# Thirteen ways to pass from the output projection of one block to the input projection of the next

## The chip, the cores and the metric

The kernel runs on one core of a Trainium2 chip. The metric is the device time of one execution in microseconds (us); the median of several runs is compared. TensorE appears in the profile as PE (matmuls) and PEld (weight loads), VectorE as DVE, ScalarE as ACT, GpSimd as POOL, and SyncE, which issues the large DMAs, as SP.

## The reference, cut to what matters

Two layers are computed on 256 rows of 1024 channels. Each layer has a feed-forward network (FFN), a token mixer and a second FFN, so there are four FFNs:

```
def swiglu(x, w_in, w_out):
    gate, up = jnp.split(x @ w_in, 2, axis=-1)
    return (jax.nn.silu(gate) * up) @ w_out

for l in range(2):
    x = layer_norm(alpha * x + 0.5 * swiglu(x, w_ff1_in[l], w_ff1_out[l]), ...)
    x = layer_norm(alpha * x + hybrid_mixer(x, ...), ...)
    x = layer_norm(alpha * x + 0.5 * swiglu(x, w_ff2_in[l], w_ff2_out[l]), ...)
```

The inner width of an FFN is 4096. All of it is float32.

## The kernel before, in words

**Precision.** A float32 product is made of three matmuls of a shorter type. Each operand is split into `hi` and `lo` (line 90 on ACT rounds, line 91 on DVE subtracts), and hi times hi, hi times lo and lo times hi are added up in PSUM. Each matmul has a weight load of its own, of 128 by 128.

**Input projection.** An FFN is cut into 32 units of 128 gate and 128 up columns. For one unit `wide` calls `mm3` sixteen times (two column groups, eight slices of the 1024 channels), so that a unit is 48 matmuls of 256 columns, on lines 185, 186 and 187 in turn. Their output tile is called `mm` or `sm`. `gate` then makes silu(gate) times up, and `split` leaves `g[u]` as a `hi` and a `lo`.

**Output projection.** After every second unit a block `j` follows, which adds the product of `g[2j]`, `g[2j+1]` and two weight tiles to the four accumulators `acc` (two row tiles by two halves of 512 columns). `rows` issues it: 2 units by 2 row tiles by 3 products by 2 halves, 24 matmuls of 512 columns, all on line 203. With `NLAST = 6` there are 13 such blocks in an FFN, 52 in the kernel. Block 12 is followed by four units without a block, and the last six `g` are multiplied in `finish`. The first three units of an FFN (two in the very first) are made in another way, by lines 286 to 288 with transposes on line 253.

**Order.** One list of instructions goes to each engine. A planner puts them in order from the program's order and from when it thinks that an operand is there. In the steady part of an FFN the trace shows the program's own order: 96 matmuls of two units, then 24 of the block, and so on. At the start of an FFN it shows pieces of the first block among the units.

**Data.** `Ring.chunk` fetches 1 MB of weights by a DMA on SP's queue into a tile `raw` and splits it into two pairs of `hi` and `lo`, which have five buffers each.

Of the kernel before, what the change touches and what calls it, by code (L numbers as in the profile page):

```python
# [77 lines left out]
class Ring:  # L78
    def __init__(self, nc, pool):
        self.nc = nc  # L80
        self.pool = pool
# [28 lines left out]
PGT = ("vv", "vv", "vg")  # L110
PBR = ("vv", "vv", "vg")
ORDER = "K0 G4 B0 K1 G5 C0 K2 B1 K3 G7 k V0 G8 G6 V1 C1 G9 v i s G10 B2 C2 G11 G0 B3 G1 Z0 G2 Z1 G3 p R1 R2 R0"


class Build:
    def __init__(self, nc, tc, pool, psum, dram, a):
        self.nc, self.tc, self.pool, self.psum, self.a = nc, tc, pool, psum, a
        self.ring = Ring(nc, pool)
        self.con = pool.tile([128, NCONST], F32, name="con")
        self.sums = pool.tile([128, NSUM], F32R, name="sums")  # L120
        self.nh = pool.tile([128, 16], F32, name="nh")
        nc.vector.memset(self.nh, -0.5)
        self.en = pool.tile([128, 8], F32, name="en")
        nc.vector.memset(self.en, float(np.e))
        self.dram = [dram.tile([8, 128, 16], F32, tag=f"d{i}", name=f"d{i}") for i in range(3)]
        self.ident = self.con[:, C_ID:C_ID + 128]
        self.xx = pool.tile([128, 8, 2, S], F32R, name="xhl")
        self.xh, self.xl = self.xx[:, :, 0], self.xx[:, :, 1]
        self.xs = [[x[:, k] for k in range(8)] for x in (self.xh, self.xl)]
        self.x = pool.tile([128, 2, D], F32, name="x")  # L130
# [50 lines left out]
            nc.sync.dma_start(out=self.x[:, t], in_=self.a["x"][t * 128:(t + 1) * 128, :])  # L181

    def mm3(self, out, wh, wl, xh, xl, start, stop):
        mm = self.nc.tensor.matmul
        mm(out, wh, xh, start=start, stop=False)  # L185
        mm(out, wh, xl, start=False, stop=False)  # L186
        mm(out, wl, xh, start=False, stop=stop)  # L187

    def wide(self, out, w, xh, xl, nk):
        n = 0  # L190
        for hi, lo in w:
            for o in range(0, hi.shape[1], 128):
                ct, k = divmod(n, nk)
                self.mm3(out[:, ct], hi[:, o:o + 128], lo[:, o:o + 128], xh[k], xl[k], k == 0, k == nk - 1)
                n += 1
# [20 lines left out]
    def ffn(self, wi, wo, lnp, first, last):  # L216
        nc = self.nc
        if not first:
            lng = self.load_ln(lnp)
        acc = None  # L220
        g = []

        def gate(gg, gate, up):
            s = self.tl(list(gg.shape), "cv")
            nc.scalar.activation(out=s, in_=gate, func=AF.Silu)
            nc.vector.tensor_tensor(out=gg, in0=s, in1=up, op=ALU.mult)  # L226

        n0 = 2 if first else NFIRST
        if first:
            ps = self.first(wi)  # L230
            for u in range(2):
                gg = self.tl([128, S], "th")
                gate(gg, ps[2 * u], ps[2 * u + 1])
                t = self.tl([128, 2, S], "g", F32R)
                self.split(t[:, 0], t[:, 1], gg)
                g.append((t[:, 0], t[:, 1]))
        else:
            tags = (OTHER + (RING,) * 4)[:2 * n0]
            ws, ps = [], []
            for u in range(n0):  # L240
                ws.append(self.ring.chunk(wi[u], tags=tags[2 * u:2 * u + 2], engs=self.engs(PFF[2 * u:2 * u + 2])))
                ps.append(self.ps([128, 2, S], "acc" if u < 2 else "mm"))
                g.append(self.tl([128, 2, S], "g", F32R))
            for t in range(2):
                c = slice(t * 128, t * 128 + 128)
                for u in range(n0):
                    for k in range(8):
                        hi, lo = [w[:, (k % 4) * S:(k % 4) * S + S] for w in ws[u][k // 4]]
                        self.mm3r(ps[u][:, t], self.xs[0][k][:, c], self.xs[1][k][:, c], hi, lo, k == 0, k == 7)
                    gg = self.tl([128, 128], "th")  # L250
                    gate(gg, ps[u][:, t, 0:128], ps[u][:, t, 128:256])
                    tp = self.ps([128, 128], "sm")
                    nc.tensor.transpose(tp, gg, self.ident)
                    self.split(g[u][:, 0, c], g[u][:, 1, c], tp)
            g = [(t[:, 0], t[:, 1]) for t in g]
        for u in range(n0, 32):
            w = self.ring.chunk(wi[u])
            if first and u in (6, 10):
                with self.tc.issue_after(self.ring.last.ins):
                    if u == 6:  # L260
                        self.second()
                    else:
                        lng = self.load_ln(lnp, nc.sync)
            gg = self.tl([128, S], "th")
            ps = self.ps([128, 2, S], ("mm", "sm")[u // 2 % 2])
            self.wide(ps, w, self.xs[0], self.xs[1], 8)
            gate(gg, ps[:, 0], ps[:, 1])
            t = self.tl([128, 2, S], "g", F32R)
            self.split(t[:, 0], t[:, 1], gg)
            g.append((t[:, 0], t[:, 1]))  # L270
            j = u // 2 - 1
            if u % 2 == 1 and u >= 3 and 2 * j < 32 - NLAST:
                if acc is None:
                    acc = [[self.ps([128, 512], "acc") for h in range(2)] for t in range(2)]
                for i, w in enumerate(self.ring.chunk(wo[j])):
                    for t in range(2):
                        self.rows(acc[t], t, g[2 * j + i], w, j == 0 and i == 0, False)
        tags = (EXTRA + (RING,) * 4)[:NLAST]
        ws = []
        for n in range(NLAST // 2):  # L280
            ws += self.ring.chunk(wo[16 - NLAST // 2 + n], tags=tags[2 * n:2 * n + 2])
        self.finish(acc, g[32 - NLAST:], ws, 0.5, lng, last)
# [51 lines left out]
    def mixer(self, l):  # L334
# [438 lines left out]
        def step(n):  # L773
            k, j = n[0], int(n[1:] or 0)
            if k == "K":
                conv(proj(j), j, [put_kq(j, 0), put_kq(j, 1)])
            elif k == "V":
                values_a(4 + j)
            elif k == "B":
                head_b(j)  # L780
            elif k == "C":
                proj_c(12 + j)
            elif k == "G":
                gates(j // 4, j % 4)
            elif k == "Z":
                if j == 0:
                    self.z2 = tl([128, 4, S], "vz")
                silu2(6 + j)
            elif k == "R":
                branch(j, (lambda: [(oa[:, 0, h], oa[:, 1, h]) for h in range(4)], lambda: kept(obb), lambda: kept(oc))[j]())  # L790
            else:
                dict(k=keys, v=values_t, i=inverse, s=scan, p=post)[k]()

        for n in ORDER.split():
            step(n)
# [11 lines left out]
        for j in range(4):  # L807
# [6 lines left out]
            st=2, mv=2, ve=2, rs=2, nm=4, sum=4, rsum=4, es=4)  # L814
# [78 lines left out]
```

## Time and profile before

| | us |
|---|---|
| median of three runs | 1664.85 |
| lowest and highest of the three | 1662.47, 1664.9 |
| the profiled execution's own time | 1666.97 |
| its span, first to last instruction | 1665.2 |

The profile is of one execution. Its busy times are unions of the records of an engine; matmuls overlap in the records, and their ends are modelled, so that the spacing of starts tells how fast TensorE goes, and the duration of a record does not.

### The profile page before, as it was taken

Reading aid. Unit: us, or ns where it says so; the run is one execution under the profiler, and the core shown is the slowest. Engines: PE = TensorE matmul, PEld = TensorE weight load, DVE = VectorE, ACT = ScalarE, POOL = GpSimd, SP = SyncE. Lnnn points to the kernel's source line nnn. Section 1 sums busy time; section 2 is a strip of 40 time slices with the busy share of each in tenths; the row PEclk is TensorE's granted clock in tenths of the full one; section 3 lists DMA queues with packets and bytes.
Section 4 is the critical chain, followed back from the end, with each engine's and each line's share of the span. In section 5 each row is a group of like instructions: output and inputs, shape, how many; then the busy total and the mean of one; then the engine's idle time right before and its main releaser. Section 6 shows DMA issues by size and latency. Waiting matters only on the chain.

```text
span 1665.2 us, 29265 instructions
## 1 busy us (share of the span) xinstructions
PE 1641.8 (99%) x12238; PEld 1533.0 (92%) x12238; DVE 1046.4 (63%) x1580; ACT 791.7 (48%) x1297; POOL 175.4 (11%) x145
## 2 busy tenths in 40 slices
PE   8999999999999999999999999999999999999998
PEld 7999998999889899999899999989988889999997
DVE  6555555889669755555655555567886696555555
ACT  5444443675444444444444444536754444444442
POOL 0000001123014300000210000011320152000000
PEclk9999999999999999999999999999999999999999
DMA  8655553544335555555555555535353355555552
GB/s 323 214 200 179 195 201 123 213 147 153 129 135 188 187 193 196 183 191 189 187 192 182 199 179 200 195 134 209 141 161 122 107 201 179 205 195 183 192 188 77
DMA packets 52342, 298.28 MB, mean 179 GB/s; under 512 B 11601, under 2 KB 13521, under 8 KB 18673
## 3 DMA queue, kind: packets, MB, share of 16 engines
q1 hardware_dynamic: 50208, 289.39, 48.8%
q0 software_dynamic: 2000, 7.01, 1.3%
q8 instruction: 96, 1.57, 0.4%
q14 instruction: 38, 0.30, 0.1%
HBM read 294.94 MB, written 1.44 MB: 178 GB/s over the span
## 4 chain that ended last, share of the span: by engine, by line
PE 93%; DVE 4%; ACT 1%; DMA 1%; issue 0%; SPq 0%; POOL 0%; DVEq 0%; ACTq 0%; POOLq 0%
PE acc L203 25%; PE mm L185 13%; PE mm L187 12%; PE mm L186 12%; PE sm L185 7%; PE sm L187 7%; PE sm L186 7%; DVE lo L91 2%; PE acc L288 1%; PE acc L286 1%; PE acc L287 1%; PE acc L670 1%; PE sm L500 1%; PE sm L551 1%; PE sm L492 1%; PE sm L499 1%
## 5 line engine op out<-in xcount | busy, mean ns | idle before, releaser
L91 DVE TENSOR_TENSOR lo<-raw,hi 128x1024 fp32r<-128x1024 f32 (+1 forms) x498 | 618.3, 1247 | 488.3 <-ACT hi L90 487.4
L90 ACT ACTIVATE hi<-raw 128x1024 fp32r<-128x1024 f32 (+1 forms) x542 | 564.0, 1049 | 668.4 <-PE mm L186 210.0
L185 PE MATMUL mm<-xhl,hi 128*128 128x256 f32 x1744 | 491.9, 282 | 0.0
L186 PE MATMUL mm<-xhl,hi 128*128 128x256 f32 x1744 | 490.3, 281 | 0.0
L187 PE MATMUL mm<-xhl,lo 128*128 128x256 f32 x1744 | 489.7, 281 | 0.0
L187 PEld LDWEIGHTS mm<-xhl,lo 128*128 128x128 f32 x1744 | 332.6, 191 | 3.2 <-issue 2.4
L185 PEld LDWEIGHTS mm<-xhl,hi 128*128 128x128 f32 x1744 | 329.1, 189 | 5.7 <-issue 4.2
L186 PEld LDWEIGHTS mm<-xhl,hi 128*128 128x128 f32 x1744 | 329.2, 189 | 3.1 <-issue 1.8
L203 PE MATMUL acc<-hi,g 128*128 128x512 f32 x1152 | 324.6, 390 | 0.0
L185 PE MATMUL sm<-xhl,hi 128*128 128x256 f32 x976 | 274.4, 281 | 0.8 <-ACT hi L90 0.8
L187 PE MATMUL sm<-xhl,lo 128*128 128x256 f32 x976 | 274.2, 281 | 0.8 <-DVE lo L91 0.8
L186 PE MATMUL sm<-xhl,hi 128*128 128x256 f32 x976 | 274.1, 281 | 0.0
L203 PEld LDWEIGHTS acc<-hi,g 128*128 128x128 f32 x1152 | 211.3, 188 | 41.2 <-ACT g L143 0.7
L187 PEld LDWEIGHTS sm<-xhl,lo 128*128 128x128 f32 x976 | 187.2, 192 | 1.0 <-DVE lo L91 1.0
L185 PEld LDWEIGHTS sm<-xhl,hi 128*128 128x128 f32 x976 | 183.2, 188 | 1.9 <-ACT hi L90 1.0
L186 PEld LDWEIGHTS sm<-xhl,hi 128*128 128x128 f32 x976 | 183.3, 188 | 0.9
L203 PE MATMUL acc<-lo,g 128*128 128x512 f32 x576 | 182.7, 389 | 0.0
L91 POOL TENSOR_TENSOR lo<-raw,hi 128x1024 fp32r<-128x1024 f32 (+1 forms) x44 | 104.0, 2377 | 372.3 <-ACT hi L90 369.5
L203 PEld LDWEIGHTS acc<-lo,g 128*128 128x128 f32 x576 | 108.1, 188 | 22.6
L309 POOL TENSOR_TENSOR rs<-ve,nh 128x1 f32<-128x1 f32 x12 | 11.8, 984 | 782.9 <-DVE ve L307 782.9
L145 DVE TENSOR_TENSOR g<-th,g 128x256 fp32r<-128x256 f32 x119 | 51.0, 428 | 2.1 <-ACT g L143 1.9
L143 ACT ACTIVATE g<-th 128x256 fp32r<-128x256 f32 x119 | 47.9, 402 | 4.4 <-DVE th L226 4.4
(237 smaller groups left out, 1564.2 us busy)
## 6 DMA issues: line engine op xcount, KB each, us to landing
raw<-w2i SPq DMA_DIRECT2D x64, 1024.0 KB, 4.8
raw<-w1i SPq DMA_DIRECT2D x62, 1024.0 KB, 4.8
raw<-w1o SPq DMA_DIRECT2D x32, 1024.0 KB, 4.9
raw<-w2o SPq DMA_DIRECT2D x32, 1024.0 KB, 4.8
raw<-wg SPq DMA_DIRECT2D x28, 1024.0 KB, 4.8
raw<-wgt SPq DMA_DIRECT2D x24, 1024.0 KB, 5.0
raw<-wbr SPq DMA_DIRECT2D x12, 1024.0 KB, 4.8
raw<-wout SPq DMA_DIRECT2D x8, 1024.0 KB, 4.8
```

The source lines that it names most:

```text
L90: nc.scalar.activation(out=hi, in_=raw, func=AF.Copy)
L91: (eng or nc.vector).tensor_tensor(out=lo, in0=raw, in1=hi.bitcast(F32), op=ALU.subtract)
L143: nc.scalar.activation(out=hi, in_=src, func=AF.Copy, scale=scale)
L145: nc.vector.tensor_tensor(out=lo, in0=src, in1=hi.bitcast(F32), op=ALU.subtract)
L185: mm(out, wh, xh, start=start, stop=False)
L186: mm(out, wh, xl, start=False, stop=False)
L187: mm(out, wl, xh, start=False, stop=stop)
L203: mm(acc[h], x[:, c], y[:, h * n:h * n + n], start=start and i == 0, stop=stop and i == 2)
L286: mm(out, xh, wh, start=start, stop=False)
L287: mm(out, xh, wl, start=False, stop=False)
L288: mm(out, xl, wh, start=False, stop=stop)
L492: T.transpose(pt[:, i], s[:, i * 128:i * 128 + 128], self.ident)
```

## The change

The 24 matmuls of a block are made by a new function, `block`, which can keep back the last few of them. The function `mm`, through which `mm3` now issues, counts the matmuls of the next unit and emits a held one as soon as the count reaches its number. A form such as (2, 2) means that the last two of the block's matmuls come after the second input-projection matmul of the next unit; (3, 6) puts one after the third and one after the sixth. The form "first" holds nothing, and makes the next unit's first matmul as two of 128 columns; "rows" makes the block's last matmul as two of 256 columns. The form () changes nothing. Block `j` of FFN number `nffn` has form `(j + 3 * nffn) % 13`, so that each form is used once in each FFN, four times in all. What is computed is the same.

```
+FORMS = ((), (2, 2), (1, 1), (3, 3), (1,), (2,), (3,), (2, 2, 2), (2, 2, 2, 2), (3,) * 6, (3, 6), "first", "rows")
...
+        self.held, self.done, self.halves, self.nffn = [], 0, False, 0
...
     def mm3(self, out, wh, wl, xh, xl, start, stop):
-        mm = self.nc.tensor.matmul
+        mm = self.mm
...
+    def mm(self, out, w, x, start, stop):
+        mm = self.nc.tensor.matmul
+        if self.halves:
+            for c in (slice(0, 128), slice(128, 256)):
+                mm(out[:, c], w, x[:, c], start=start and c.start == 0, stop=stop)
+            self.halves = False
+        else:
+            mm(out, w, x, start=start, stop=stop)
+        self.done += 1
+        while self.held and self.held[0][0] <= self.done:
+            self.held.pop(0)[1]()
+
+    def block(self, acc, gs, ws, start, form):
+        mm = self.nc.tensor.matmul
+        todo = []
+        for i, (g, w) in enumerate(zip(gs, ws)):
+            for t in range(2):
+                c = slice(t * 128, t * 128 + 128)
+                for p, (x, y) in enumerate(((g[0], w[0]), (g[0], w[1]), (g[1], w[0]))):
+                    for h in range(2):
+                        todo.append((acc[t][h], x[:, c], y[:, h * 512:h * 512 + 512], start and i == 0 and p == 0))
+        after = form if isinstance(form, tuple) else ()
+        n = len(todo) - len(after)
+        for q, (o, x, y, st) in enumerate(todo[:n]):
+            if form == "rows" and q == n - 1:
+                for d in (slice(0, 256), slice(256, 512)):
+                    mm(o[:, d], x, y[:, d], start=st, stop=False)
+            else:
+                mm(o, x, y, start=st, stop=False)
+        self.done = 0
+        self.held = [(a, lambda o=o, x=x, y=y, st=st: mm(o, x, y, start=st, stop=False)) for a, (o, x, y, st) in zip(after, todo[n:])]
+        self.halves = form == "first"
...
-                for i, w in enumerate(self.ring.chunk(wo[j])):
-                    for t in range(2):
-                        self.rows(acc[t], t, g[2 * j + i], w, j == 0 and i == 0, False)
+                self.block(acc, g[2 * j:2 * j + 2], self.ring.chunk(wo[j]), j == 0, FORMS[(j + 3 * self.nffn) % len(FORMS)])
+        self.nffn += 1
```

## Rows read from the trace of the kernel before

**Rows 1.** The page: busy time by engine.

```profile
PE 1641.8 (99%) x12238; PEld 1533.0 (92%) x12238; DVE 1046.4 (63%) x1580; ACT 791.7 (48%) x1297; POOL 175.4 (11%) x145
```

**Rows 2.** Stretches: length, busy PE, PEld, DVE, ACT, POOL (instructions), clock, DMA.

```profile
607.11:618.42 11.31, 11.31 (x98) 11.31 (x96) 5.76 (x7) 4.82 (x6) 0.00 (x0) 1.00 0.53 188
618.42:623.86 5.44, 5.44 (x27) 4.51 (x25) 2.93 (x4) 2.70 (x4) 0.00 (x0) 1.00 0.57 193
866.03:875.32 9.29, 9.29 (x84) 9.29 (x83) 7.19 (x9) 5.28 (x9) 0.00 (x0) 1.00 0.62 228
601.63:607.11 5.48, 5.48 (x26) 4.50 (x25) 2.92 (x4) 2.69 (x4) 0.00 (x0) 1.00 0.56 193
875.32:880.78 5.46, 5.46 (x27) 4.51 (x25) 3.01 (x5) 2.70 (x4) 0.00 (x0) 1.00 0.56 195
1358.33:1363.85 5.52, 5.52 (x49) 5.52 (x47) 5.49 (x7) 1.66 (x5) 4.00 (x2) 1.00 0.93 371
1411.66:1417.20 5.54, 5.54 (x49) 5.54 (x48) 1.52 (x2) 1.34 (x2) 0.00 (x0) 1.00 0.00 0
```

**Rows 3.** PE in order of time, 865 to 875: start, us, line, tiles, shape, count.

```profile
864.99 0.63 PE L203 MATMUL acc<-hi,g 128*128 128x512 f32 x2
865.45 0.28 PE L185 MATMUL mm<-xhl,hi 128*128 128x256 f32 x1
...
866.03 0.28 PE L187 MATMUL mm<-xhl,lo 128*128 128x256 f32 x1
...
875.21 0.28 PE L187 MATMUL mm<-xhl,lo 128*128 128x256 f32 x1
```

**Rows 4.** Groups by line, PE, 866.2 to 875.2: count, busy us, mean ns.

```profile
L187 PE MATMUL mm<-xhl,lo 128*128 128x256 f32 x27 | 7.5, 276 | 0.0
```

**Rows 5.** PE in order of time, 582 to 586.

```profile
582.00 0.28 PE L185 MATMUL mm<-xhl,hi 128*128 128x256 f32 x1
...
582.23 0.63 PE L203 MATMUL acc<-hi,g 128*128 128x512 f32 x2
582.70 0.62 PE L203 MATMUL acc<-lo,g 128*128 128x512 f32 x2
583.16 0.28 PE L187 MATMUL mm<-xhl,lo 128*128 128x256 f32 x1
...
584.69 0.28 PE L185 MATMUL mm<-xhl,hi 128*128 128x256 f32 x1
584.81 0.27 PE L253 MATMUL sm<-con,th 128*128 128x128 f32 x1
...
585.04 0.28 PE L186 MATMUL sm<-xhl,hi 128*128 128x256 f32 x1
...
585.50 0.28 PE L187 MATMUL sm<-xhl,lo 128*128 128x256 f32 x1
...
585.96 0.28 PE L185 MATMUL sm<-xhl,hi 128*128 128x256 f32 x1
```

**Rows 6.** PE in order of time, 857 to 860.

```profile
857.69 0.27 PE L253 MATMUL sm<-con,th 128*128 128x128 f32 x1
857.72 0.71 PE L203 MATMUL acc<-hi,g 128*128 128x512 f32 x2
858.27 0.63 PE L203 MATMUL acc<-lo,g 128*128 128x512 f32 x2
858.74 0.28 PE L187 MATMUL mm<-xhl,lo 128*128 128x256 f32 x1
...
859.10 0.28 PE L187 MATMUL mm<-xhl,lo 128*128 128x256 f32 x1
...
859.55 0.28 PE L185 MATMUL sm<-xhl,hi 128*128 128x256 f32 x1
```

**Rows 7.** PE in order of time, at 1411.

```profile
1411.44 0.27 PE L253 MATMUL sm<-con,th 128*128 128x128 f32 x1
```

**Rows 8.** Groups by line, PE, 1358.4 to 1363.8: count, busy us, mean ns.

```profile
L186 PE MATMUL mm<-kq,hi 128*128 128x256 f32 x16 | 4.5, 283 | 0.0
```

## The prediction

> **What bounds the kernel now.** I read the page first. PE is busy in 99% of the span; DVE is at 63% and ACT at 48% [rows 1]. A busy PE can still lose time, so the next view is that of stretches. In the steady FFN two units, 96 matmuls of 256 columns, take 11.31 us, and the block's 24 of 512 take 5.44 us, with PE busy throughout and DVE and ACT at about half [rows 2]. Every ns that PE saves there therefore comes off the end, until some other engine falls behind, and those two have half of their time free.
>
> Then I asked how far apart the starts are. 11.31/96 = 117.8 ns for 256 columns and 5.44/24 = 226.7 ns for 512. Half of 226.7 is 113.3, so the narrow matmul loses 4.5 ns against the 512-column one. It need not: from 866.03 to 875.21 the same matmuls of the same lines, 81 of them (one of three rows with 27 each is shown [rows 4]), take 9.18 us, 113.3 ns [rows 3]. The granted clock is 1.00 in both stretches, the 2.4 GHz level, and PE is busy all through both [rows 2]. So TensorE runs the same work at two spacings that each persist: **wide-spaced**, 117.8, and **close**, 113.3. The reader should see that neither the operands nor the clock tells them apart; only what came just before does.
>
> The Trainium skill, page "TensorE: Matmul & The Clock Gate", section "Back-to-back issue gap", has one gap for one size, N/2.4 + 2.5 ns, which is 109 ns for 256 columns. By that page what precedes a matmul doesn't matter and this change can only add the cost of its extra instructions. The trace does not agree, with 113.3 and 117.8 for one size at one clock.
>
> **What sets the spacing.** Three findings, all from starts in order of time.
>
> (a) A block left after its 24 matmuls always leads to wide-spaced units: so it does at 607.11, and even where it was entered from close ones, at 875.32. That entry costs 5.46 - 5.44 = 0.02 us [rows 2].
>
> (b) A block entered after 96 wide-spaced matmuls goes at 226.7 from its first one. But after two such, at 582.23, four 512-column matmuls take 0.93 us where 4 x 226.7 = 0.91 [rows 5]; and the block at 601.63, entered after 80 (units 3 to 5 are 144; 2, 14 and 48 had gone before), takes 5.48 [rows 2]. 96 is a multiple of three, 2 and 80 are two more than one. I read the wide spacing as a cycle of three matmuls: at its start a 512-column matmul fits without loss, two matmuls later it is out of step and loses some 5 ns each until it is back.
>
> (c) Where PE leaves a run of 512-column matmuls out of step, units can be close. At 864.99 two of them are entered from close ones, and the units after them are close again by 866.03 [rows 3]. At 857.72 a transpose and four 512-column ones lead to three input-projection matmuls in 0.36 us (120 ns each), and from 859.10 to 859.55 four take 0.45, close [rows 6]. Against that, the four at 582.23 lead to 13 matmuls in 1.53 us, wide-spaced [rows 5].
>
> A short foreign matmul is not reliable: the transpose at 584.81 is followed by close units (four in 0.46 us from 585.50), while the same sequence at 1411.44 [rows 7] is followed by 47 (a unit's 48 less the first) in 5.54, 117.9 ns [rows 2].
>
> **The change part by part.** Nothing is removed. The same 24 matmuls and 48 a unit are issued, but for 8 more: four for "first", four for "rows". No DMA is added or moved past another on SP's or POOL's queue; a block's fetch and split are emitted before the block as ever. What moves is the release of one pair of weight buffers, by at most six matmuls of 113 to 118 ns, 0.7 us. Behind it waits ACT's rounding of a pair several halves of a chunk ahead, then DVE's subtraction; with ACT and DVE busy for 4.82 and 5.76 of 11.31 us that is hidden [rows 2]. If it were not, it would cost up to 0.7 us a block. The held matmuls' inputs are older than those of the units around them, so they bring no wait.
>
> *The price of a flip.* I say that a form flips PE where the units behind it are close. A close unit pair saves 96 x 4.5 = 0.43 us, less the few matmuls before it settles (0.02), less 0.02 for the next block's entry, less up to 0.02 for held ones out of step: 0.38 us. Behind block 12 stand four units and it saves twice that. Where a form doesn't flip but breaks the count of three, it costs 0.02 for its held matmuls and 5.48 - 5.44 = 0.04 at the next block: 0.06 us.
>
> The forms, four blocks each:
>
> - (): 0.
> - (3, 3), (3,), six times 3, (3, 6): held after a multiple of three, so in step by (b): 0. Bounds: 0.06 lost to 0.38 gained per block.
> - (2, 2, 2, 2): at 582.23 as it stands: wide-spaced. +0.06.
> - (2, 2, 2): no row is the same. The first three of the four at 857.72 come nearest, because there PE leaves out of step and goes close. I take a flip.
> - (2, 2): two out of step, as at 864.99: a flip. The other end is the wide-spaced one at 582.23.
> - (2,), (1,), (1, 1): one or two 512-column ones out of step; after one narrow matmul no row shows the loss. Two of three endings in (c) are close, two of these three would be; I take one, because none is like them.
> - "first": an extra matmul of 128 columns. The transpose and the matmul after it take 585.04 - 584.81 = 0.23 us where 0.12 is normal: +0.11. Flip or not is one against one [rows 5, 7]; I take the flip.
> - "rows": two of 256 columns at 113 to 118 each for one at 227: 0 to 9 ns, and no flip, since these are just two more of the 256-column kind, which break the count: +0.05.
>
> *Sum.* Four forms flip, 16 blocks: -16 x 0.38 = -6.1, and -0.3 for a flipped block 12 (of the four forms that stand there, "rows", (1, 1), (2,) and (2, 2, 2, 2), one is taken). "first": 4 x 0.11 = +0.4. The other four that break the count: 16 x 0.06 = +1.0. Together -5.0 us. On the profiled execution's own 1666.97 that is 1662.0; that execution lies 2.1 us above the median of the runs, so for the median I forecast 1664.85 - 5.0, about 1660.
>
> **The rivals.** 0.2% of this kernel, 3.3 us, is about what a measurement can tell from no change.
>
> *The wide spacing takes everything.* PE falls back to 117.8 after any interleaving, as at 582.23, or the spacing depends on something that order doesn't reach. Then only costs remain: seven forms, 28 blocks at 0.06 and 0.4 for "first", +2.1 us: 1667. The 52 blocks that all end so speak for it; the two places in (c) against. The page named above would give +0.5, for the extra instructions, 1665.4. With two or three flips it is -1 to -3 us. All of this is no measurable change: 0.34.
>
> *Nearly everything flips.* Six or seven forms, or the multiples of three too. 28 x 0.38 = 10.6 less 0.4 and more for block 12: 1654. With all 48 it would be 18 less: 1647. For it: close units last once entered, 81 matmuls and on. Against it: (b). 0.18, most of it near 1654.
>
> *A third spacing, the case on the other side.* In the last branch before the mixer's output projection the same lines run at 5.52/46 = 120.0 ns (47 matmuls touch the stretch, 16, 16 and 15 by line, one begun before it) [rows 2, 8]. If interleaving left PE there, a unit pair would lose 96 x 2.2 = 0.21 us; 28 blocks lose 5.9, with the costs above 8: 1673. It becomes measurable from some 16 blocks on. Against it: these units read another tile, and no unit of an FFN shows it. 0.06.
>
> *The order doesn't come out.* The planner takes a held matmul at once if it believes the next unit's weights to be late, as it put pieces of the first block among units at 582.23 [rows 5]. Then nothing changes: 1665, 0.04. In the steady part the order is the program's.
>
> **How the numbers follow.** My forecast, four or five forms flipping, has 0.38, with 1657 to 1661 as its own range. Faster: 0.38 + 0.18 and little of the rest, 0.56. The same: 0.34 + 0.04, 0.38. Slower: 0.06. The range for 8 in 10 goes from 1653, which takes in the seven forms, to 1667, where no form flips.
>
> **What would show it.** In the profile after, starts of line 185 to 187 matmuls behind each block: 96 in 10.9 us where a form flips, 11.31 where not, the same at all four places of a form. The blocks after a flip take 5.46, those after a broken count 5.48. Forms with 3 should show no loss at all. DVE, ACT and DMA should not change, and PE should have no new gap. I am wrong if units behind (2, 2) and (2, 2, 2) stay at 117.8, if one form behaves differently at its four places, or if the mixers, whose spacing also depends on what came before, move by more than a us or two.

## The result, and the profile after

The changed kernel takes 1656.46 us (median of four runs, 1655.34 to 1657.91), the one before 1664.88 in the same comparison: a ratio of 0.995, with a 95% interval from 0.9933 to 0.9968. It is 8.4 us faster; 1660.0 was forecast, in a range of 1653 to 1667. The profiled execution of after has 1655.71 us.

The page's busy row, which answers to [rows 1], moves on TensorE alone (PE and PEld); DVE, ACT and POOL do the same work in the same time.

```profile
PE 1630.6 (99%) x12246; PEld 1521.2 (92%) x12246; DVE 1046.1 (63%) x1580; ACT 791.4 (48%) x1297; POOL 175.1 (11%) x145
```

Eight more instructions on PE, and 11.2 us less busy. Next the view of stretches of after, as in [rows 2]: length, busy PE, PEld, DVE, ACT, POOL (instructions), clock, DMA share, GB/s. Each row but those of blocks runs from the first unit matmul behind the last held one to the start of the next block. In order of the rows: units behind (); the block after them; units behind (2, 2); the block after those; then units behind (3, 3), behind (1,) and the block after them, behind (2, 2, 2, 2), and the four units behind "rows".

```profile
36.64:47.95 11.31, 11.31 (x97) 11.30 (x96) 5.77 (x7) 5.23 (x7) 0.00 (x0) 1.00 0.82 324
47.95:52.94 4.99, 4.99 (x25) 4.13 (x23) 2.47 (x3) 2.70 (x4) 0.00 (x0) 1.00 0.62 215
53.64:64.30 10.66, 10.66 (x95) 10.66 (x94) 5.48 (x6) 4.82 (x6) 0.00 (x0) 1.00 0.54 197
64.30:69.30 5.00, 5.00 (x24) 4.14 (x23) 2.56 (x4) 2.70 (x4) 0.00 (x0) 1.00 0.82 275
86.48:97.43 10.95, 10.95 (x94) 10.95 (x93) 5.57 (x6) 4.82 (x6) 0.00 (x0) 1.00 0.54 193
103.00:114.19 11.19, 11.19 (x97) 11.19 (x95) 5.63 (x7) 4.82 (x6) 0.00 (x0) 1.00 0.52 189
114.19:119.42 5.23, 5.23 (x25) 4.32 (x24) 2.69 (x3) 2.69 (x4) 0.00 (x0) 1.00 0.56 201
169.81:180.88 11.07, 11.07 (x95) 11.06 (x94) 5.57 (x6) 4.82 (x6) 0.00 (x0) 1.00 0.52 191
236.28:258.06 21.78, 21.78 (x195) 21.78 (x194) 15.54 (x19) 13.48 (x18) 0.00 (x0) 1.00 0.66 236
```

Behind (2, 2, 2, 2), 94 unit matmuls take 11.07 us, 117.8 ns each; behind (2, 2), 94 of them take 10.66, 113.4, and so they do behind "rows" (192 in 21.78). The clock is 1.00 in all of them, the 2.4 GHz level. Read so, the thirteen forms fall into two groups, the same at every place in the steady part of an FFN. Close units follow (2, 2), (1, 1), (2, 2, 2), "first" and "rows"; wide-spaced ones follow (), (3, 3), (3,), six times 3, (3, 6), (1,), (2,) and (2, 2, 2, 2). Five forms flip, 20 blocks. Behind block 12 two of them stand ("rows" and (1, 1)), so that 22 unit pairs run close.

The order of PE around a held pair, form (2, 2): start, us, line, tiles, shape, count. Line 198 makes the matmuls of the units, 221 the held ones and 217 the pieces of a cut one.

```profile
52.94 0.40 PE L198 MATMUL sm<-xhl,hi 128*128 128x256 f32 x2
53.17 0.63 PE L221 MATMUL acc<-hi,g 128*128 128x512 f32 x2
53.64 0.28 PE L198 MATMUL sm<-xhl,lo 128*128 128x256 f32 x1
```

Two unit matmuls take 0.23 us and the two held ones 0.47, where two in step take 0.45: they are out of step, and PE leaves them close. Around the cut matmul of "rows":

```profile
236.04 0.40 PE L217 MATMUL acc<-hi,g 128*128 128x256 f32 x2
236.28 0.40 PE L198 MATMUL mm<-xhl,hi 128*128 128x256 f32 x2
236.52 0.28 PE L198 MATMUL mm<-xhl,lo 128*128 128x256 f32 x1
236.63 0.39 PE L198 MATMUL mm<-xhl,hi 128*128 128x256 f32 x2
236.86 0.28 PE L198 MATMUL mm<-xhl,lo 128*128 128x256 f32 x1
```

The two pieces take 0.24 us, the first two unit matmuls 0.24 (120 ns each), and by 236.63 they are close: two in 0.23, and 192 in 21.78 as a whole.

### The profile page after: what moved, and what is told of

The parts are those of the page before. It is cut to its first block, busy times and chain, and to the rows that moved or that the text cites. A ratio compares the mean times of both kernels' runs of the same rounds, so it can differ in the third digit from the quotient of the medians.

```text
span 1653.9 us, 29281 instructions
## 1 busy us (share of the span) xinstructions
PE 1630.6 (99%) x12246; PEld 1521.2 (92%) x12246; DVE 1046.1 (63%) x1580; ACT 791.4 (48%) x1297; POOL 175.1 (11%) x145
## 4 chain that ended last, share of the span: by engine, by line
PE 91%; DVE 5%; DMA 1%; ACT 1%; issue 1%; SPq 0%; POOL 0%; DVEq 0%; ACTq 0%; POOLq 0%
PE mm L198 36%; PE sm L198 20%; PE acc L219 16%; PE acc L238 8%; DVE lo L91 2%; PE acc L221 1%; DMA raw<-w1i 1%; PE acc L322 1%; PE acc L320 1%; PE acc L704 1%; PE acc L321 1%; PE sm L534 1%; PE sm L585 1%; ACT hi L90 1%; PE sm L526 1%; DVE cv L478 1%
## 5 line engine op out<-in xcount | busy, mean ns | idle before, releaser
L198 PE MATMUL mm<-xhl,hi 128*128 128x256 f32 x3486 | 619.6, 280 | 0.0
L198 PEld LDWEIGHTS mm<-xhl,hi 128*128 128x128 f32 x3486 | 533.8, 188 | 9.0 <-issue 5.8
L198 PE MATMUL sm<-xhl,hi 128*128 128x256 f32 x1950 | 341.5, 279 | 0.8 <-ACT hi L90 0.8
L198 PEld LDWEIGHTS sm<-xhl,hi 128*128 128x128 f32 x1950 | 298.4, 188 | 3.4 <-ACT hi L90 1.0
L219 PE MATMUL acc<-hi,g 128*128 128x512 f32 x752 | 209.5, 390 | 0.0
L219 PEld LDWEIGHTS acc<-hi,g 128*128 128x128 f32 x752 | 137.0, 188 | 25.1
L219 PE MATMUL acc<-lo,g 128*128 128x512 f32 x396 | 122.4, 389 | 0.0
L238 PE MATMUL acc<-hi,g 128*128 128x512 f32 x320 | 92.8, 392 | 0.0
L219 PEld LDWEIGHTS acc<-lo,g 128*128 128x128 f32 x396 | 74.3, 188 | 15.8
L238 PEld LDWEIGHTS acc<-hi,g 128*128 128x128 f32 x320 | 59.3, 188 | 13.3 <-DVE g L149 0.7
L238 PE MATMUL acc<-lo,g 128*128 128x512 f32 x160 | 54.6, 390 | 0.0
L478 DVE SCALAR_TENSOR_TENSOR cv<-cin,par,cv 128x256 f32<-128x256 f32 x72 | 41.7, 625 | 0.2
```

Source lines behind the costliest of these rows:

```text
L198: mm(out, w, x, start=start, stop=stop)
L219: mm(o, x, y, start=st, stop=False)
L238: mm(acc[h], x[:, c], y[:, h * n:h * n + n], start=start and i == 0, stop=stop and i == 2)
L478: V.scalar_tensor_tensor(out=cv, in0=cin[:, q:q + S], scalar=w[:, q:q + 1], in1=cv, op0=ALU.mult, op1=ALU.add)
```

## The experiments

Diffs are against the changed kernel; where a kernel goes without `block` and `mm`, against the kernel before. Times are in us; a single time is one execution, the kernel before is the one beside it.

**One form everywhere.** The first, (2, 2) at every block, asks whether the price of a flip adds up; the second, (3, 3), whether a multiple of three is free.

```
-FORMS = ((), (2, 2), (1, 1), (3, 3), (1,), ...)
+FORMS = ((2, 2),)        # the other kernel: ((3, 3),)
```

> All 52 blocks take the form (2, 2). Theory (the count of three sets the spacing, and a pair of 512-column matmuls after the second narrow one flips PE to the 113.3 ns spacing every time): 52 unit pairs and the 4 extra pairs behind block 12 save 0.38 us each, 21 us: 1643.6 us, up to 1645 if the planner scatters block 0 of three FFNs. Rival (the 8.4 us came from the mixers and from the start, which also ran differently, and a flip is worth little): no more than 10 us below the kernel before, 1655 or above.

> All 52 blocks take the form (3, 3). Theory: held after a multiple of three the pair is in step, units stay at 117.8 ns, a block's matmuls at 226.7 without loss, and the time is that of the kernel before, 1665 within 2 us. Rival (what helps is that two 512-column matmuls stand among narrow ones at all, so that a weight load gets ahead): units at 113.3 and some 20 us saved, 1645.

With (2, 2) the time is 1644.98 (1642.55 to 1646.97; before 1664.17), ratio 0.9886 (0.9871 to 0.99). It adds up: 49 pairs are close, and 4 more behind block 12, which at 0.38 us each are 20.1; the medians are 19.2 apart. With (3, 3) it is 1665.41, ratio 1.0002 (0.9992 to 1.0011): held matmuls as such cost nothing. The stretches of the first show a steady place, and the units after block 0 of the second FFN:

```profile
52.38:63.04 10.66, 10.66 (x95) 10.66 (x94) 5.49 (x6) 4.82 (x6) 0.00 (x0) 1.00 0.57 197
583.99:593.42 9.43, 9.43 (x82) 9.43 (x81) 7.75 (x10) 5.42 (x8) 0.00 (x0) 1.00 0.78 308
```

At 583.99, 80 unit matmuls take 9.43 us, 117.8 ns: there the planner has scattered the block's matmuls among the units, and no pair of them leaves PE out of step. Behind block 0 it is so in each of the last three FFNs (80, 87 and 80 matmuls).

**Where the count of three ends.** The pair is held back further into the next units.

```
+FORMS = ((), (4, 4), (5, 5), (6, 6), (7, 7), (8, 8), (9, 9), (10, 10), (20, 20), (21, 21), (22, 22), (47, 47), (48, 48))
```

> Thirteen forms again: (), then a pair of 512-column matmuls held until after the 4th, 5th, 6th, 7th, 8th, 9th, 10th, 20th, 21st, 22nd, 47th and 48th narrow matmul. Theory (count modulo three): the units behind 4, 5, 7, 8, 10, 20, 22 and 47 go to 113.3 ns, those behind 6, 9, 21 and 48 stay at 117.8; about 32 flips of 0.4 down to 0.2 us: 1653 to 1655. Rival (what counts is nearness to the block, with weight loads or waits still in the queue): no flip from 4 on, and 1665; or a flip behind all of them but ().

One execution: 1650.84 (before 1664.17). Units are close behind a pair held after 4, 5, 7, 8, 10, 20, 22 and 47, and wide-spaced behind one after 6, 9, 21 and 48. Stretches behind 20, 21, 47 and 48:

```profile
171.10:179.72 8.62, 8.62 (x78) 8.62 (x76) 5.40 (x6) 4.71 (x6) 0.00 (x0) 1.00 0.53 201
187.65:196.48 8.83, 8.83 (x76) 8.83 (x75) 5.48 (x6) 4.71 (x6) 0.00 (x0) 1.00 0.51 194
223.93:229.49 5.56, 5.56 (x50) 5.56 (x49) 4.17 (x5) 3.44 (x5) 0.00 (x0) 1.00 0.38 138
240.60:257.56 16.96, 16.96 (x145) 16.96 (x144) 13.80 (x17) 11.22 (x17) 0.00 (x0) 1.00 0.60 207
```

76 in 8.62 us are 113.4 ns, 75 in 8.83 are 117.7; 49 in 5.56 are 113.5, 144 in 16.96 are 117.8. One matmul more or less decides, 48 matmuls after the block as well as three.

**How many held ones it takes.**

```
+FORMS = ((2,) * 5, (2,) * 6, (2,) * 7, (2,) * 8, (2,) * 9, (2,) * 10, (1,) * 3, (1,) * 4, (1,) * 5, (1,) * 6, (2, 2), (1, 1), ())
```

> Thirteen forms: after the second narrow matmul 5, 6, 7, 8, 9 or 10 held ones; after the first 3, 4, 5 or 6; then (2, 2), (1, 1) and (). Theory (a pair flips because PE leaves the 512-column matmuls before they are back in step): from 9 on behind the second, and from 3 on behind the first, the run is back at 226.7 and the units stay at 117.8; 5 to 8 behind the second are still out of step, and at least two of them flip. Rival (a second run of 512-column matmuls behind an uneven count flips whatever its length): all of them flip but ().

One execution: 1662.58 (before 1664.35). Stretches behind seven, eight and nine held after 2, and behind three held after 1:

```profile
70.35:81.42 11.07, 11.07 (x95) 11.06 (x94) 5.57 (x6) 4.82 (x6) 0.00 (x0) 1.00 0.67 243
87.14:97.80 10.66, 10.66 (x95) 10.66 (x94) 5.49 (x6) 4.82 (x6) 0.00 (x0) 1.00 0.58 198
103.53:114.61 11.08, 11.08 (x96) 11.07 (x95) 5.57 (x6) 4.82 (x6) 0.00 (x0) 1.00 0.52 191
137.02:148.21 11.19, 11.19 (x96) 11.19 (x95) 5.63 (x7) 4.82 (x6) 0.00 (x0) 1.00 0.53 190
```

With the forms of after, two, three, five, six and eight 512-column matmuls held after 2 flip PE; one, four, seven, nine and ten don't. After 1, two flip; one and three to six don't. By their starts, held ones are back at 226 to 227 ns from the tenth after 2 and from the fourth after 1. A run that stops there or one short of it flips nothing, nor does one that stops after the first, and, after 2, the fourth or the seventh: again steps of three.

**Do the three products make the three?** Two kernels ask whether the count comes from the order hi-hi, hi-lo, lo-hi. In the first all three products read the same operands; in the second one product is left out, so that a unit pair is 64 matmuls.

```
         mm(out, wh, xh, start=start, stop=False)
-        mm(out, wh, xl, start=False, stop=False)
-        mm(out, wl, xh, start=False, stop=stop)
+        mm(out, wh, xh, start=False, stop=False)
+        mm(out, wh, xh, start=False, stop=stop)
...
# the other kernel
         mm(out, wh, xh, start=start, stop=False)
-        mm(out, wh, xl, start=False, stop=False)
         mm(out, wl, xh, start=False, stop=stop)
```

> The kernel before, with all three matmuls of an input projection (and of the mixers' projections) made on the same operands, hi weights and hi inputs; the two products with a lo part are left out of the result. If the cycle of three comes from the three products reading different places: the cycle is gone, with one spacing for all, and an entry into a block either always or never loses. If it is the array's own timing: units behind a block stay at 117.8 ns with the same pattern and the time stays at 1665. If all went at 113.3: some 25 us less, 1640.

> The kernel before without the product of hi weights and lo inputs in every projection, so that a unit is 32 matmuls and two units are 64, one more than a multiple of three. Theory (the cycle of three is the array's own): behind a block the units still go at 117.8, and every block entered after 64 of them loses 20 to 25 ns at its start (239, 232, 231) instead of none. Rival (the cycle is that of the three products): no loss at the entry, or another spacing than 117.8. The time falls by a third of the units in either case, to about 1330 if PE still sets it, more if the splitting on DVE does.

The first took 1676.0 (before 1664.17), the second 1431.59 (before 1664.35), one execution each. Stretches of the first, 96 unit matmuls and the block behind them:

```profile
52.80:64.11 11.31, 11.31 (x98) 11.31 (x97) 5.66 (x6) 4.82 (x6) 0.00 (x0) 1.00 0.50 185
64.11:69.55 5.44, 5.44 (x27) 4.50 (x26) 3.21 (x4) 2.69 (x4) 0.00 (x0) 1.00 0.82 270
```

Nothing has changed there: 117.8 ns, and no loss at the block. Its extra time lies elsewhere: between the profiled executions, some 6 us in each of the two mixers and none in the FFNs. Part of that is the clock, with a granted clock of 0.50 for 10.2 us of the first mixer and 6.8 us of the second, where the kernel before has 3.4 in each; that is at most 5 of the 12 us, and where the rest comes from wasn't followed. In the second, the block after 64 unit matmuls, and the 64 after it:

```profile
42.83:48.29 5.46, 5.46 (x26) 4.52 (x25) 2.23 (x5) 2.52 (x4) 0.00 (x0) 1.00 1.02 419
48.29:55.83 7.54, 7.54 (x65) 7.53 (x64) 6.45 (x7) 5.12 (x7) 0.00 (x0) 1.00 0.74 273
```

64 is one more than a multiple of three, and now every block enters with a loss, 5.46 instead of 5.44; the units stay at 117.8. The count belongs to matmuls, not to the products. The time itself was expected at about 1330 if PE set it; PE is busy for 94% of that run and the granted clock is 0.956 on average, and where the other 100 us go wasn't followed.

**Why "rows" flips.** This form went against the prediction. The first kernel cuts the block's last matmuls in other ways: the halves exchanged ("back"), two or three cut, a whole one or more behind the cut one ("then1", "then2", "then6"), both halves into one half of the accumulator ("low", "high"), 384 and 128 columns, and the last twelve cut.

```
+CUTS = {"last": {-1: ((0, 256), (256, 512))}, "back": {-1: ((256, 512), (0, 256))}, ...,
+        "then6": {-7: ((0, 256), (256, 512))}, "low": {-1: ((0, 256, 0), (256, 512, 0))}, ...,
+        "all256": {-q: ((0, 256), (256, 512)) for q in range(1, 13)}}
+FORMS = ((),) + tuple(CUTS)
...
+            for d in cut.get(q - n, ((0, 512),)):
+                dd = d[2] if len(d) > 2 else d[0]
+                mm(o[:, dd:dd + d[1] - d[0]], x, y[:, d[0]:d[1]], start=st, stop=False)
```

> Thirteen forms in which nothing is held and matmuls at a block's end are cut: () ; the last one as two of 256 columns (last), in the other order of halves (back); the last two or three, or the last twelve, each as two of 256; the one before the last (then1), the third last (then2) or the seventh last (then6) as two of 256; the last as two of 256 that both write the low half or both the high half of the accumulator (low, high: here a product goes to the wrong columns and one half goes without it); the last as 384 and 128, or 128 and 384 columns. Theory of the destination (a 256-column matmul that follows one into the other half of its bank goes at 113.3, one that follows one into the same half at 117.8): last, back, two, three, twelve flip the units behind them, low and high do not. Theory of the operands (it is the reading of other tiles by the cut matmul that shifts the step): low and high flip as last does. Both: then6 leaves the array back in step, units at 117.8; then1 and then2 leave it out of step, and at least one of them flips.

One execution: 1650.87 (before 1664.35). All but () and "then6" flip. Stretches behind "then2" and "then6", then the order of PE at the end of "all256":

```profile
136.15:147.04 10.89, 10.89 (x97) 10.89 (x96) 5.65 (x7) 4.82 (x6) 0.00 (x0) 1.00 0.56 195
152.53:163.84 11.31, 11.31 (x98) 11.31 (x96) 5.73 (x7) 4.82 (x6) 0.00 (x0) 1.00 0.52 187
```

```profile
232.58 0.64 PE L223 MATMUL acc<-lo,g 128*128 128x256 f32 x4
233.06 1.12 PE L223 MATMUL acc<-hi,g 128*128 128x256 f32 x8
234.02 0.64 PE L223 MATMUL acc<-lo,g 128*128 128x256 f32 x4
```

Six whole matmuls behind the cut one bring the block back in step, and nothing flips. "low" and "high" flip like "last", so which half of the accumulator the pieces write has no part. And the pieces themselves go at a spacing of their own: four from 232.58 to 233.06, eight from 233.06 to 234.02, 120.0 ns each. They are 256 columns, as a unit's are, but they read their moving operand from the weights ring, not from the input tile `xhl`.

The destination was tried in the units too, with two column groups of a unit in turn:

```
+        for k in range(nk):
+            for p in range(3):
+                for ct in range(2):
+                    hi, lo = cols[ct * nk + k]
+                    mm(out[:, ct], (hi, hi, lo)[p], (xh, xl, xh)[p][k], ...)
```

> The kernel before, with the two column groups of a unit taken in turn, matmul by matmul, so that each narrow matmul writes the other half of its PSUM bank than the one before it. Theory of the destination: no unit goes at 117.8 any more, all at 113.3, some 25 us less, 1640. Theory of the array's own timing (the cycle of three follows from the lengths of load and matmul alone): the units behind a block stay at 117.8 and the time at 1665, within 5 us for the mixers' order.

1674.75 (1673.0 to 1678.62; before 1664.35), ratio 1.0063 (1.0042 to 1.0085). The units stay at 117.8 ns (96 in 11.30 us), with no loss at the block:

```profile
53.84:65.14 11.30, 11.30 (x97) 11.30 (x96) 4.53 (x6) 3.85 (x6) 0.00 (x0) 1.00 0.53 194
```

The destination falls, and the other theory's time, 1665 within 5 us, was missed too. Between the profiled executions, 3.2 and 2.8 us of what it loses lie in the mixers, which call the same function.

In the kernel with (2, 2) everywhere the two held matmuls share their stationary operand (what PEld loads). Another order at the block's end gives them two different ones, and asks whether that matters:

```
+FORMS = ((2, 2),)
...
+        todo[-3], todo[-2] = todo[-2], todo[-3]
```

> All blocks (2, 2), but with the order at the block's end changed so that the two held matmuls have different weights and the same accumulator (lo weights with hi inputs, then hi with lo, both in the second half), where before they had the same weights and two accumulators. Theory (only number and step count): units at 113.3 behind every block as with all blocks (2, 2), 1645. Rival (the pair flips because the second needs no new weights, or goes to another bank): units at 117.8, 1665.

1645.94 in one execution (before 1665.5), and every steady place flips as with (2, 2) alone. Whether the two share it has no part.

**"rows" at every block.**

```
+FORMS = ("rows",)
```

> All 52 blocks take the form rows: the last matmul is cut in two of 256 columns, nothing is held. The forms of the cut run showed it flip behind block 0 of the later FFNs too, where (2, 2) does not. Theory: 52 pairs and 4 more behind block 12 at 0.38 us each, 21.5 us below the kernel before, 1643, about 1 us better than all blocks (2, 2) and hardly to be told from it. Rival (cutting only flips when the forms vary, or it costs as much as it gives): 1655 or above.

1643.31 (1642.58 to 1646.7; before 1665.5), ratio 0.9872 (0.9856 to 0.9888): the best version here, beside (2, 2) everywhere, whose interval overlaps. Stretches of a steady place and of the one behind block 0 that (2, 2) couldn't reach:

```profile
55.32:66.22 10.90, 10.90 (x98) 10.90 (x97) 5.67 (x7) 4.82 (x6) 0.00 (x0) 1.00 0.53 192
588.91:598.00 9.09, 9.09 (x83) 9.09 (x82) 7.67 (x10) 5.41 (x8) 0.00 (x0) 1.00 0.78 306
```

Here the 80 matmuls behind block 0 take 9.09 us, 113.6 ns: a cut needs no unit beside it, so the planner's scatter doesn't undo it.

**Which operand of the pieces counts.** The last matmul is replaced by pieces whose stationary operand is from `g` or from the ring, and whose moving operand is from the ring or from `xhl`. "gr", "g0r", "ghr", "rr" and "r1r" move the ring, "gx", "gxx", "rx" and "r1x" move `xhl`, and three forms, "one", "onex" and "oner", issue one piece instead of two.

```
+PIECES = {"gr": (("g", "r0", 0), ("g", "r1", 1)), ...,
+          "gx": (("g", "x", 0), ("g", "xl", 1)), ..., "rr": (("r", "r0", 0), ("r", "r1", 1)), ...,
+          "rx": (("r", "x", 0), ("r", "xl", 1)), ...}
...
+                for u, m, h in PIECES[form]:
+                    u = {"g": g[1][:, 128:256], ..., "r": w[0][:, 0:128], ...}[u]
+                    m = {"r0": w[0][:, 512:768], ..., "x": self.xh[:, 0], ...}[m]
+                    mm(o[:, h * 256:h * 256 + 256], u, m, start=st, stop=False)
```

> Thirteen forms: (), and twelve in which the last matmul of a block is replaced by one or two of 256 columns with other operands, so that part of that product is missing and something else is added to the accumulator. Weights from g (lo or hi, two places) or from the ring of weights (two places), inputs from the ring or from the unit's own input tile. Theory of the moving operand: what reads the ring (gr, g0r, ghr, rr, r1r) flips, what reads the input tile as a unit does (gx, gxx, rx, r1x) stays at 117.8. Theory of the weights: g flips (gr, g0r, ghr, gx, gxx), ring weights do not (rr, r1r, rx, r1x). Theory of the count: every pair flips whatever it reads, and the single ones (one, onex, oner) do not. The time is between 1645 and 1660.

One execution: 1657.38 (before 1665.5). Stretches behind "gr", "gx", "rr" and "rx":

```profile
55.19:66.09 10.90, 10.90 (x99) 10.90 (x97) 5.67 (x7) 4.83 (x6) 0.00 (x0) 1.00 0.54 192
104.27:115.58 11.31, 11.31 (x99) 11.31 (x97) 5.76 (x7) 4.82 (x6) 0.00 (x0) 1.00 0.56 187
137.87:148.77 10.90, 10.90 (x99) 10.90 (x98) 5.67 (x7) 4.82 (x6) 0.00 (x0) 1.00 0.54 195
170.59:181.90 11.31, 11.31 (x99) 11.31 (x97) 5.75 (x7) 4.82 (x6) 0.00 (x0) 1.00 0.56 188
```

All five forms that move the ring flip; the four that move `xhl` don't, whichever the stationary operand is, and no single piece does. Pieces that move `xhl` are what the prediction took the pieces of "rows" for: two more of the units' kind. Those of "rows" are not. All the stationary operands here, `g` and the ring, begin at the same place modulo 512 bytes as the ring that moves; so this run doesn't tell the moving operand by itself from how the two operands lie to each other.

**The place of the tiles.** What differs between the ring and `xhl` is where they lie. The last run moves tiles in SBUF and keeps every instruction of the run above. `xhl` moves by 96 bytes, the ring, `g` and `kq` by 32. (`pq` was made behind `xhl` before.)

```
-        self.en = pool.tile([128, 8], F32, name="en")
+        self.en = pool.tile([128, 16], F32, name="en")[:, 0:8]
...
+        self.pq = self.tl([128, 16], "pq")
         self.xx = pool.tile([128, 8, 2, S], F32R, name="xhl")
```

> The kernel of 'sources' with two tiles laid out otherwise and not one instruction changed: a small tile in front gets 32 bytes more, and another 64 bytes move ahead of the input tile. By the built program's addresses, the input tile, the weights ring and g then begin at a multiple of 64 bytes (in all kernels before: 32 off one), and the input tile and the ring at the same place modulo 1024 bytes (64; before, 992 and 32). As in 'sources', the last matmul of blocks is replaced, so the computed result changes there. Theory A, the 32 bytes make the wide spacing: the units are at 113.3 ns (or one other spacing) everywhere, also behind (); with 113.3 about 1644 us. Theory B, the ring's matmuls step otherwise than the input tile's because of their place modulo 1024 bytes: gr, g0r, ghr, rr, r1r and gx, gxx, rx, r1x now do the same, all flip (about 1651 us) or none (about 1665). Theory C, neither has a part: just as 'sources', the five that read the ring flip, the others don't, about 1657 us. I give C 0.5, A 0.25, B 0.25.

1689.32 (1688.7 to 1690.58; before 1665.63), ratio 1.0143 (1.0125 to 1.0162), 32 us more than the same instructions took in the run above. Stretches: the block entered from units, the units behind "gr", behind "gx", behind "one":

```profile
49.13:54.60 5.47, 5.47 (x27) 4.55 (x26) 2.93 (x4) 2.69 (x4) 0.00 (x0) 1.00 0.56 196
54.60:66.12 11.52, 11.52 (x98) 11.52 (x97) 5.76 (x7) 4.82 (x6) 0.00 (x0) 1.00 0.50 182
105.58:117.10 11.52, 11.52 (x98) 11.52 (x97) 5.76 (x7) 4.82 (x6) 0.00 (x0) 1.00 0.53 183
207.42:218.94 11.52, 11.52 (x98) 11.52 (x97) 5.88 (x7) 4.82 (x6) 0.00 (x0) 1.00 0.53 183
```

96 in 11.52 us are 120.0 ns, behind every form and also behind (): the cycle of three is gone, and no form does anything. None of the three theories had this time. C falls: the place of the tiles sets the spacing. A and B each had a half that came out (one other spacing everywhere; all forms alike), but neither that it would be 120.0. Since the 32 bytes and the place modulo 1024 were changed in one run, this run doesn't part them; rows of other kernels do. The tile `kq`, 32 off a multiple of 64 and at 32 modulo 1024, goes at 120.0 too [rows 2, 8], and so do the ring's pieces in "all256", at the same place; so 120.0 comes with the 32 bytes and without. Nor is it the place of the moving operand alone. In the first units of an FFN (lines 286 to 288 of the kernel before) the operands change roles: the ring moves and `xhl` is stationary. Two stretches of such matmuls in the kernel before, 29 and 30 from start to start, and then 29 in the kernel with moved tiles:

```profile
565.20:568.49 3.29, 3.29 (x31) 3.29 (x30) 3.16 (x7) 0.31 (x2) 1.03 (x2) 1.00 0.75 299
575.39:578.92 3.53, 3.53 (x32) 3.53 (x31) 2.65 (x6) 2.27 (x4) 0.00 (x0) 1.00 0.49 158
572.82:576.30 3.48, 3.48 (x31) 3.48 (x30) 3.13 (x7) 0.28 (x2) 1.24 (x2) 1.00 0.72 283
```

They go at 113.4 and 117.7 ns, with the ring where it is for the 120.0 of "all256", and at 120.0 once the tiles are moved. What goes with 120.0 in all these rows is that both operands begin at the same place modulo 512 bytes (slices of a stationary operand are 512 apart): the ring with `kq` or `g`, at 32 in the built program, and in the last kernel the ring with `xhl`, at 64. Where the ring and `xhl` lie 64 bytes apart, whichever of them moves, it is 113.3 or 117.8, by what went before. This is read from rows that differ in more than that; no run moved one tile alone.

## Why the prediction was right, and where it was not

**The bound.** It held: PE is busy for 99% and every ns saved on it came off the end; the other engines' busy times and the DMA's packets did not move.

**Two spacings, and the three findings.** (a) and (b) held to the ns: after () units are wide-spaced, after (3, 3) they are too and nothing is lost, and the count of three reaches at least to 48 matmuls, as the pair held after 47 and 48 shows. (c) held as the general way to flip: PE must leave a short run of 512-column matmuls out of step. The prediction had this as a reading of five places; the runs show it, and with it the exceptions, by how many are out of step. One row goes past the count: behind (2, 2, 2, 2) the next block loses nothing after 94 wide-spaced matmuls (18 of its matmuls in 4.08 us), one more than a multiple of three.

**The price.** 0.38 us a pair. Measured: 94 matmuls take 10.66 where 11.07 is wide-spaced, 0.41 less; the next block takes 5.00 instead of 4.99, and the two held ones 0.47 instead of 0.45. That leaves 0.38.

**The forms.** For (), the four with 3, (2, 2), (2, 2, 2), (2, 2, 2, 2) and "first" the forecast came out, and of (2,), (1,) and (1, 1) just one flips, as taken. For these three and for "first" no row decided, so that they came out was luck. One step failed, that of "rows": "no flip, since these are just two more of the 256-column kind, which break the count". They are not of the units' kind: they move the ring, and such pieces flip PE, while pieces that move `xhl` behave as the step says. The form flips at all its four places.

**The sum.** With its own prices and the flips as they came: 22 pairs by 0.38 are 8.4 us; "first" costs 0.4, its halves and the matmul behind them 0.11 each time as forecast; (1,) and (2,) cost 0.03 to 0.04 a block (5.23 for 23 matmuls of the next block where 23 x 226.7 is 5.21, and 0.01 at the held one), (2, 2, 2, 2) 0.02, where 0.06 was taken. Together -7.6 instead of -5.0: "rows" gave 2.1 of the difference (five pairs, and the 0.05 a block that it was to cost), the smaller costs most of the rest. Measured are -8.4 between the medians, with -5.3 to -11.2 by the interval. Between the two profiled executions the span is 11.3 us shorter: 0.7 ahead of the first block, 9.3 in the FFNs, 0.1 and 1.2 in the two mixers, within the "us or two" that the prediction allowed. Some of that is not the change but the clock. These are the first units of the third FFN, the same 156 instructions of PE ahead of its blocks, in the kernel before and then in after:

```profile
832.38:853.12 20.74, 19.96 (x156) 19.76 (x156) 11.75 (x22) 6.87 (x15) 5.34 (x4) 0.92 0.40 143
827.37:846.72 19.35, 18.57 (x156) 18.36 (x156) 11.77 (x22) 6.87 (x15) 5.34 (x4) 1.00 0.43 152
```

In the execution before, the granted clock is 0.50, the 1.2 GHz level, from 834.53 to 837.94, behind two waits of PE, across which starts lie 1.36 and 1.06 us apart; in after, PE has the same two waits there and the clock stays at 1.00. The second mixer of before has another 3.4 us at 0.50, from 1223.65, and that of after has none; its 1.2 us go along with that. Without the 1.4 us above, the FFNs are 7.9 shorter, against 7.6 from the sum.

**The rivals.** The wide spacing didn't take everything back: the order reaches it, at least where `xhl` lies as it does. Nearly everything flipping did not happen either, as multiples of three are free of it. The third spacing, 120.0, came after no form of the change; but it is real for the units, as the run with the moved tiles shows, and the prediction's reason against it ("these units read another tile") was the right place to look. There it costs 96 x 2.2 ns a pair and 0.03 at each block, 13 us in the 56 pairs and 52 blocks; of the 24 us in all, some 8 lie in the mixers by the profiled executions.

The Trainium skill, page "TensorE: Matmul & The Clock Gate", section "Back-to-back issue gap", gives N/2.4 + 2.5 ns, 109 ns for 256 columns, as the gap of a single matmul taken alone; it adds that in a stream of weight loads and matmuls both set the spacing, and has 131 ns for 512 columns there. The prediction took the first as the Trainium skill's rule for such a stream. No run here agrees with either. At a granted clock of 1.00, 512 columns go at 226.7 ns, and the same 256 columns at 113.3, 117.8 or 120.0, by what went before and by where the operands lie. The kernels here that lie furthest apart in it, 1643 and 1689 us, differ by 46 us, of which 56 pairs of 96 at 113.3 and at 120.0 make some 36.

## What to carry to other kernels

Where an engine is busy for 99%, divide a stretch's length by its matmuls, and compare the same instructions at two places: here 4% of a spacing hid in a row that looked full. If two spacings show, look for what PE leaves behind just before each, and try the smallest break there; cutting the last 512-column matmul of a block in two was one line and took 1.3% off. Its time can't be told from that of (2, 2) everywhere, but it also reached the three places where the planner had scattered the held pair. A kernel tuned so is tied to where its tiles lie: moving the input tile by 96 bytes, and the ring and `g` by 32, took all of it away and 24 us more, so a change of a buffer's size, though no instruction differs, is to be timed.

## What the runs showed of the hardware

- Units, runs of matmuls of 256 columns, have three spacings at a granted clock of 1.00: 113.3, 117.8 and 120.0 ns. (A run on a tile at yet another place, `oc` in the mixers before, goes at 118.7 in the first layer and at 117.3 in the second.) At 2.4 GHz these are 272, 282.7 and 288 cycles, and 512 columns (226.7 ns) are 544. Three at 117.8 are 848 cycles, as much as one of 272 and two of 288; that the cycle of three is made of these is a guess from the sum, and the starts (117, 118, 118, 119 ns) don't show it.
- The spacing is kept for as long as the run lasts (192 matmuls close, 192 wide-spaced), until a foreign shape comes; a run of 512-column matmuls is back in step after three to nine of them.
- The same instructions go otherwise when their tiles are moved by some bytes: 1657 us and 1689. Runs of 256-column matmuls went at 120.0 where both operands begin at the same place modulo 512 bytes, and at 113.3 or 117.8 where they lie 64 bytes apart. Which places give 113.3 by themselves wasn't tried; and why the ring's pieces set the units behind them close is open: shown is that pieces that move the ring do, and those that move `xhl` don't.
- Two executions can differ by the clock alone: the same 156 instructions of PE, behind the same waits, took 20.74 us at a mean granted clock of 0.92 and 19.35 at 1.00.
- In the mixers, two kernels that keep the FFNs' spacing took 6 to 12 us more than before (the one with column groups in turn, the one with equal products), part of the second by the clock. Why wasn't taken apart.
